# Adaptive max pooling on one core: a nine-row ring, 48 KB load runs, 9 KB store runs, and stores queued behind the last load

## The chip, the cores and the metric

One core of one Trainium2 chip. The metric is the device time of one execution in microseconds (us), lower is better. The profile's "span" is the time from the first to the last instruction of one profiled execution; it is 1.7 to 1.8 us shorter than the time of the same execution, so spans are compared with spans and times with times. All runs told here were in the fast state (none is set apart as slow by a lower clock or a longer time), at a granted clock of 1.0. A ratio is the mean time of one kernel's fast runs over that of the other's fast runs of the same rounds, so it is not quite the ratio of the medians quoted beside it.

## The reference

The input is float32 of 32 x 256 x 4096. Each row of 4096 is cut into 256 windows of 16, and each window gives its maximum:

```python
for i in range(output_size):                    # 256
    start = int(i * length / output_size)       # 16 * i
    end = int((i + 1) * length / output_size)
    result[:, :, i] = np.max(x[:, :, start:end], axis=-1)
```

There are 8192 rows, 64 for each of the 128 SBUF partitions. 134.2 MB are read and 8.39 MB written, with one pass of maxima over the input.

## The kernel before

A partition gets two consecutive rows per load (32 KB contiguous) in one of three buffers. VectorE reduces each row, and each pair of rows is stored (2 KB contiguous per partition). The first 14 stores go out on ScalarE's DMA queue when they are ready. The next 16 are deferred and put on SyncE's queue, the one that issues the loads, in groups of 6, 5 and 5. The last four rows are loaded in smaller pieces.

```python
R = 2; IN_BUFS = 3; CHUNKS_PER_ROW = 4; N_CHUNK_ROWS = 2; N_FULL_ROWS = 2
DEF_A, DEF_B, DEF_C = 6, 5, 5
xt = xf.rearrange("(n p r) (o w) -> n p r o w", p=P, r=R, w=W)
ot = of.rearrange("(n p r) m -> n p (r m)", p=P, r=R)
# ... pools and helpers cut ...
for n in range(n_body):                          # 30 loads of two rows
    t = in_pool.tile([P, R, O, W], fp32, tag="in")
    nc.sync.dma_start(out=t, in_=xt[n])
    o = new_out()
    for r in range(R):
        nc.vector.reduce_max(out=o[:, r * O : (r + 1) * O], in_=t[:, r],
                             axis=mybir.AxisListType.X)
    out_tiles[n] = o
    if n >= defer_start:
        deferred.append(n)
    else:
        nc.scalar.dma_start(out=ot[n], in_=o)
emit_deferred(DEF_A)
# ... two single-row loads; emit_deferred(DEF_B) ahead of the last two rows;
# ... these two rows in four pieces of 4 KB each; a store of rows 60, 61 ...
emit_deferred(len(deferred))
nc.scalar.dma_start(out=ot[last_n], in_=out_tiles[last_n])
```

Of the kernel before, what the change touches and what calls it, by code (L numbers as in the profile page):

```python
# [1 line left out]

# [4 lines left out]


@with_exitstack  # L10
def kernel(
    ctx: ExitStack,
    tc: tile.TileContext,
    x: bass.AP,
    output_size: bass.AP,
    out: bass.AP,
):
    nc = tc.nc

    B, C, L = x.shape  # L20
    O = int(output_size)
    assert L % O == 0, (L, O)
    W = L // O

    P = nc.NUM_PARTITIONS

    xf = x.flatten_outer_dims()
    of = out.flatten_outer_dims()
    rows = xf.shape[0]
    assert rows % P == 0  # L30

    fp32 = mybir.dt.float32

    R = 2
    IN_BUFS = 3
    CHUNKS_PER_ROW = 4
    N_CHUNK_ROWS = 2
    N_FULL_ROWS = 2
    DEF_A = 6
    DEF_B = 5  # L40
    DEF_C = 5

    while R > 1 and rows % (P * R) != 0:
        R //= 2
    nprow = rows // P
    nmacro = nprow // R
    n_chunks = CHUNKS_PER_ROW if O % CHUNKS_PER_ROW == 0 else 1
    oc = O // n_chunks

    n_tail_prow = min(N_CHUNK_ROWS + N_FULL_ROWS, nprow)  # L50
    n_chunk_prow = min(N_CHUNK_ROWS, n_tail_prow)
    n_tail_macro = -(-n_tail_prow // R)
    n_body = nmacro - n_tail_macro
    tail_start_prow = n_body * R
    n_defer = min(DEF_A + DEF_B + DEF_C, max(n_body - 1, 0))

    xt = xf.rearrange("(n p r) (o w) -> n p r o w", p=P, r=R, w=W)
    ot = of.rearrange("(n p r) m -> n p (r m)", p=P, r=R)

    in_pool = ctx.enter_context(tc.tile_pool(name="inpool", bufs=IN_BUFS))  # L60
    out_pool = ctx.enter_context(
        tc.tile_pool(name="outpool", bufs=min(nmacro, n_defer + 5))
    )

    out_tiles = {}
    deferred: list[int] = []

    def new_out():
        return out_pool.tile([P, R * O], fp32, tag="out", name="o")

    def emit_deferred(k):
        for _ in range(k):
            if deferred:
                m = deferred.pop(0)
                nc.sync.dma_start(out=ot[m], in_=out_tiles[m])  # L75

    defer_start = n_body - n_defer
    for n in range(n_body):
        t = in_pool.tile([P, R, O, W], fp32, tag="in")
        nc.sync.dma_start(out=t, in_=xt[n])  # L80
        o = new_out()
        for r in range(R):
            nc.vector.reduce_max(  # L83
                out=o[:, r * O : (r + 1) * O],
                in_=t[:, r],
                axis=mybir.AxisListType.X,
            )
        out_tiles[n] = o
        if n >= defer_start:
            deferred.append(n)  # L90
        else:
            nc.scalar.dma_start(out=ot[n], in_=o)

    emit_deferred(DEF_A)

    o = None
    last_n = nmacro - 1
    for q in range(tail_start_prow, nprow):
        n, r = divmod(q, R)
        if r == 0 or o is None:  # L100
            o = new_out()
            out_tiles[n] = o
        if q == nprow - n_chunk_prow:
            emit_deferred(DEF_B)
        if q < nprow - n_chunk_prow:
            tr = in_pool.tile([P, 1, O, W], fp32, tag="inrow", bufs=2)
            nc.sync.dma_start(out=tr, in_=xt[n][:, r : r + 1])
            nc.vector.reduce_max(  # L108
                out=o[:, r * O : (r + 1) * O],
                in_=tr[:, 0],  # L110
                axis=mybir.AxisListType.X,
            )
        else:
            for c in range(n_chunks):
                tl = in_pool.tile(
                    [P, oc, W], fp32, tag="inchunk", bufs=2 * n_chunks
                )
                nc.sync.dma_start(
                    out=tl, in_=xt[n][:, r, c * oc : (c + 1) * oc, :]
                )  # L120
                nc.vector.reduce_max(  # L121
                    out=o[:, r * O + c * oc : r * O + (c + 1) * oc],
                    in_=tl,
                    axis=mybir.AxisListType.X,
                )
        if r == R - 1 and n != last_n:
            nc.scalar.dma_start(out=ot[n], in_=o)

    emit_deferred(len(deferred))

    nc.scalar.dma_start(out=ot[last_n], in_=out_tiles[last_n])


# [1 line left out]
_INS = ['x', 'output_size']  # L135
_OUTS = [((32, 256, 256), 'float32')]
#: Inputs that are plain numbers.
_NUMBERS = {'output_size': 256}


# [26 lines left out]
```

## Time and profile before

| | kernel before |
|---|---|
| time, median of the first 3 runs | 339.17 us (338.6 to 339.9) |
| span of the profiled run | 336.9 us |
| VectorE (DVE) busy | 281.0 us, 83% |
| mean DMA rate over the span | 423 GB/s |
| data packets per DMA engine | 576 |

First the page of the kernel before. The row DMA has one digit for each fortieth of the span, the busy share of the 16 DMA engines in tenths; 9 is 90% or more.

```profile
span 336.9 us, 241 instructions
...
DVE 281.0 (83%) x70; POOL 0.2 (0%) x4
...
DMA  7999999999999999999999999999999999999997
...
DMA packets 10370, 142.63 MB, mean 423 GB/s; under 512 B 1152, under 2 KB 1152, under 8 KB 6272
...
L83 DVE TENSOR_REDUCE o<-t 128x256 f32<-128x4096 f32 x60 | 262.4, 4414 | 50.5 <-DMA t<-in_x_dram 50.5
```

The DMA row is full from end to end. The last line tells of VectorE: 60 reduces of 4414 ns, and 50.5 us of idle time, all ended by a load. VectorE waits for DMA.

Then the chain of waits of the kernel before, its summary line:

```profile
by line: DMA t<-in_x_dram 60.0%; DVE o L83 23.4%; DMA out_dram<-o 10.7%; DMA tl<-in_x_dram 2.8%; DVE o L121 0.7%; SPq L75 0.5%; SPq L80 0.3%; issue 0.3%; DVEq L83 0.0%
```

The chain puts 23.4% on VectorE, since each load waits for VectorE to free a buffer. But two more loads stand in the queue then, so the DMA engines don't stop. A chain shows what released what; it does not show that a queue between the two was full.

The windows of the end (bounds and length in us, busy time of VectorE and GpSimd, clock, DMA share, GB/s):

```profile
300.00:320.00 20.00, 18.08 (x5) 0.00 (x0) 1.00 0.99 401
320.00:330.00 10.00, 9.07 (x7) 0.00 (x0) 1.00 1.03 416
330.00:332.00 2.00, 1.96 (x2) 0.00 (x0) 1.00 1.04 402
332.00:334.00 2.00, 1.38 (x2) 0.00 (x0) 1.00 0.77 296
334.00:336.90 2.90, 0.00 (x0) 0.00 (x0) 1.00 0.27 102
```

In the last 5 us the engines run dry.

Each DMA packet has its own record in the trace (start, duration, size, queue). Grouped by size, for the kernel before ("sum" is over all packets, divided by 16 engines):

```
bytes   count   median ns   mean ns   sum us
 2048    4096       84         84.1    21.5
 4096    1024      159        160.3    10.3
16384     256      611        626.4    10.0
32768    3840     1213       1217.1   292.1
completion writes (4 bytes) 1152, 9 ns  0.6     all: 334.55 us
```

The medians lie on a line of 0.0368 ns per byte (0.03675 before rounding: 1213 less 84 ns over 30,720 bytes) plus 8 to 9 ns per packet. The first packet starts at 1.75 us and the last ends at 335.71 us.

### The profile page before, as it was taken

To read this page: it belongs to the slowest core of one execution; us is meant where nothing else is said; L and a number is where in the kernel's file an instruction comes from. 1 tells how busy PE (TensorE), PEld (TensorE's weight loads), DVE (VectorE), ACT (ScalarE), POOL (GpSimd) and SP (SyncE) were. 2 spreads that over 40 slices of the span, in tenths; PEclk is the share of its full clock that TensorE was granted. 3 is DMA by queue.
4 is the path that set the end of the run, shared out by engine and by line. 5 is a ranking of instruction groups with operands and counts; after the bars stand their busy time and mean duration, and the time that the engine had idled before them with its cause. 6 is when DMAs were issued, how large, how long until landed. Compare 5 with 4: busy or idle time off the path is not lost.

```text
span 336.9 us, 241 instructions
## 1 busy us (share of the span) xinstructions
DVE 281.0 (83%) x70; POOL 0.2 (0%) x4
## 2 busy tenths in 40 slices
DVE  0488988888988889888899888888988888898895
POOL 0000000000000000000000000000000000000000
DMA  7999999999999999999999999999999999999997
GB/s 311 436 436 441 417 454 406 454 409 454 426 430 430 436 428 434 430 430 435 429 438 432 436 432 436 436 436 428 424 436 428 436 412 436 429 414 427 405 414 275
DMA packets 10370, 142.63 MB, mean 423 GB/s; under 512 B 1152, under 2 KB 1152, under 8 KB 6272
## 3 DMA queue, kind: packets, MB, share of 16 engines
q1 hardware_dynamic: 8064, 138.42, 96.1%
q10 hardware_dynamic: 2304, 4.20, 3.2%
q14 instruction: 2, 0.02, 0.0%
HBM read 134.22 MB, written 8.39 MB: 423 GB/s over the span
## 4 chain that ended last, share of the span: by engine, by line
DMA 74%; DVE 24%; SPq 1%; issue 0%; DVEq 0%
DMA t<-in_x_dram 60%; DVE o L83 23%; DMA out_dram<-o 11%; DMA tl<-in_x_dram 3%; DVE o L121 1%; SPq L75 1%; SPq L80 0%; DVEq L83 0%
## 5 line engine op out<-in xcount | busy, mean ns | idle before, releaser
L83 DVE TENSOR_REDUCE o<-t 128x256 f32<-128x4096 f32 x60 | 262.4, 4414 | 50.5 <-DMA t<-in_x_dram 50.5
L121 DVE TENSOR_REDUCE o<-tl 128x64 f32<-128x1024 f32 x8 | 9.8, 1220 | 1.0 <-DMA tl<-in_x_dram 0.6
L108 DVE TENSOR_REDUCE o<-tr 128x256 f32<-128x4096 f32 x2 | 8.8, 4420 | 1.0 <-DMA tr<-in_x_dram 0.9
L148 POOL MEMSET const-bfloat16-1.0<- 128x1 bf16 x1 | 0.1, 102 | 0.0
L148 POOL MEMSET const-uint8-127<- 128x1 uint8 x1 | 0.1, 101 | 0.0
L148 POOL MEMSET const-float32-0.0<- 128x1 f32 x1 | 0.1, 99 | 0.2 <-issue 0.2
L148 POOL MEMSET const-float32-1.0<- 128x1 f32 x1 | 0.1, 98 | 0.0
## 6 DMA issues: line engine op xcount, KB each, us to landing
t<-in_x_dram SPq DMA_DIRECT2D x30, 4096.0 KB, 21.5
out_dram<-o ACTq DMA_DIRECT2D x16, 256.0 KB, 16.1
out_dram<-o SPq DMA_DIRECT2D x16, 256.0 KB, 14.0
tr<-in_x_dram SPq DMA_DIRECT2D x2, 2048.0 KB, 16.4
tl<-in_x_dram SPq DMA_DIRECT2D x8, 512.0 KB, 9.2
```

Of the source, the lines that this page charges most:

```text
L75: nc.sync.dma_start(out=ot[m], in_=out_tiles[m])
L83: nc.vector.reduce_max(out=o[:, r * O : (r + 1) * O], in_=t[:, r], axis=mybir.AxisListType.X,)
L108: nc.vector.reduce_max(out=o[:, r * O : (r + 1) * O], in_=tr[:, 0], axis=mybir.AxisListType.X,)
L121: nc.vector.reduce_max(out=o[:, r * O + c * oc : r * O + (c + 1) * oc], in_=tl, axis=mybir.AxisListType.X,)
L148: nc = _bacc.Bacc("TRN2", target_bir_lowering=False, num_devices=1)
```

## The change

The intent is fewer and larger DMA runs, with an end at which the queue holds work while VectorE finishes. Two-row buffers become a ring of nine rows filled three rows at a time (48 KB contiguous per partition). Two-row stores become nine-row stores (9 KB contiguous), seven of them. The last row, the 64th, goes in four pieces. Most group stores are held until after the last load. The words of the change say four groups; the condition holds groups 2 to 6, which is five stores.

```diff
-    R = 2
-    IN_BUFS = 3
-    CHUNKS_PER_ROW = 4
-    N_CHUNK_ROWS = 2
-    N_FULL_ROWS = 2
-    DEF_A = 6
-    DEF_B = 5
-    DEF_C = 5
+    RING = 9
+    G = 9
+    N_GROUPS = 7
+    LOAD = 3
+    LATE = [3, 2, 2, 1, 1]
+    HELD = 4
+    PIECES = 4
...  (pools: ring [P, 9, O, W], six output tiles [P, 9 * O], one last output)
+    xg = xf[0:main].rearrange("(g p r) (o w) -> g p r o w", p=P, r=G, w=W)
+    og = of[0:main].rearrange("(g p r) m -> g p (r m)", p=P, r=G)
...
+    for g in range(N_GROUPS):
+        o = outs[g % len(outs)]
+        sizes = LATE if g == N_GROUPS - 1 else [LOAD] * (G // LOAD)
+        r = 0
+        for n in sizes:
+            at = n_read % RING
+            nc.sync.dma_start(out=ring[:, at : at + n], in_=xg[g][:, r : r + n])
+            for i in range(n):
                 nc.vector.reduce_max(
+                    out=o[:, (r + i) * O : (r + i + 1) * O],
+                    in_=ring[:, at + i],
                     axis=mybir.AxisListType.X,
                 )
+            n_read += n
+            r += n
+        if g < N_GROUPS - 1 - HELD:
+            nc.scalar.dma_start(out=og[g], in_=o)
+        else:
+            held.append((og[g], o))
...  (the last row: four loads of 4 KB per partition, four reduces)
+    for dst, src in held:
+        nc.sync.dma_start(out=dst, in_=src)
+    nc.scalar.dma_start(out=ol, in_=last_out)
```

More of the change, by code (lines that the diff above doesn't have):

```diff
@@ L18 @@
     nc = tc.nc
+    P = nc.NUM_PARTITIONS
+    fp32 = mybir.dt.float32
     B, C, L = x.shape
@@ L23 @@
     W = L // O
-    P = nc.NUM_PARTITIONS
     xf = x.flatten_outer_dims()
@@ L29 @@
     rows = xf.shape[0]
-    assert rows % P == 0
-    fp32 = mybir.dt.float32
-    R = 2
-    IN_BUFS = 3
-    CHUNKS_PER_ROW = 4
-    N_CHUNK_ROWS = 2
-    N_FULL_ROWS = 2
-    DEF_A = 6
-    DEF_B = 5
-    DEF_C = 5
-    while R > 1 and rows % (P * R) != 0:
-        R //= 2
-    nprow = rows // P
-    nmacro = nprow // R
-    n_chunks = CHUNKS_PER_ROW if O % CHUNKS_PER_ROW == 0 else 1
-    oc = O // n_chunks
-    n_tail_prow = min(N_CHUNK_ROWS + N_FULL_ROWS, nprow)
-    n_chunk_prow = min(N_CHUNK_ROWS, n_tail_prow)
@@ L52 @@
-    n_tail_macro = -(-n_tail_prow // R)
-    n_body = nmacro - n_tail_macro
-    tail_start_prow = n_body * R
-    n_defer = min(DEF_A + DEF_B + DEF_C, max(n_body - 1, 0))
-    xt = xf.rearrange("(n p r) (o w) -> n p r o w", p=P, r=R, w=W)
-    ot = of.rearrange("(n p r) m -> n p (r m)", p=P, r=R)
-    in_pool = ctx.enter_context(tc.tile_pool(name="inpool", bufs=IN_BUFS))
-    out_pool = ctx.enter_context(
-        tc.tile_pool(name="outpool", bufs=min(nmacro, n_defer + 5))
-    )
-    out_tiles = {}
@@ L66 @@
-    deferred: list[int] = []
-    def new_out():
-        return out_pool.tile([P, R * O], fp32, tag="out", name="o")
-    def emit_deferred(k):
-        for _ in range(k):
-            if deferred:
-                m = deferred.pop(0)
-                nc.sync.dma_start(out=ot[m], in_=out_tiles[m])
-    defer_start = n_body - n_defer
-    for n in range(n_body):
-        t = in_pool.tile([P, R, O, W], fp32, tag="in")
-        nc.sync.dma_start(out=t, in_=xt[n])
-        o = new_out()
-        for r in range(R):
-            nc.vector.reduce_max(
-                out=o[:, r * O : (r + 1) * O],
-                in_=t[:, r],
-                axis=mybir.AxisListType.X,
-            )
-        out_tiles[n] = o
-        if n >= defer_start:
-            deferred.append(n)
-        else:
-            nc.scalar.dma_start(out=ot[n], in_=o)
@@ L94 @@
-    emit_deferred(DEF_A)
-    o = None
-    last_n = nmacro - 1
-    for q in range(tail_start_prow, nprow):
-        n, r = divmod(q, R)
-        if r == 0 or o is None:
-            o = new_out()
-            out_tiles[n] = o
-        if q == nprow - n_chunk_prow:
-            emit_deferred(DEF_B)
-        if q < nprow - n_chunk_prow:
-            tr = in_pool.tile([P, 1, O, W], fp32, tag="inrow", bufs=2)
-            nc.sync.dma_start(out=tr, in_=xt[n][:, r : r + 1])
-            nc.vector.reduce_max(
-                out=o[:, r * O : (r + 1) * O],
-                in_=tr[:, 0],
-                axis=mybir.AxisListType.X,
-            )
-        else:
-            for c in range(n_chunks):
-                tl = in_pool.tile(
-                    [P, oc, W], fp32, tag="inchunk", bufs=2 * n_chunks
-                )
-                nc.sync.dma_start(
-                    out=tl, in_=xt[n][:, r, c * oc : (c + 1) * oc, :]
-                )
+    assert rows == 64 * P
@@ new lines @@
+    RING = 9
[5 more added lines that the diff above has]
+    PIECES = 4
+    pool = ctx.enter_context(tc.tile_pool(name="pool", bufs=1))
+    ring = pool.tile([P, RING, O, W], fp32, tag="ring", name="ring")
+    outs = [
+        pool.tile([P, G * O], fp32, tag=f"out{i}", name=f"out{i}")
+        for i in range(N_GROUPS - 1)
+    ]
+    last_out = pool.tile([P, O], fp32, tag="lastout", name="lastout")
+    main = N_GROUPS * G * P
+    xg = xf[0:main].rearrange("(g p r) (o w) -> g p r o w", p=P, r=G, w=W)
@@ new lines @@
+    og = of[0:main].rearrange("(g p r) m -> g p (r m)", p=P, r=G)
+    xl = xf[main:rows].rearrange("p (o w) -> p o w", w=W)
+    ol = of[main:rows]
+    n_read = 0
+    held = []
+    for g in range(N_GROUPS):
[6 more added lines that the diff above has]
+            for i in range(n):
@@ L121 @@
                 nc.vector.reduce_max(
-                    out=o[:, r * O + c * oc : r * O + (c + 1) * oc],
-                    in_=tl,
+                    out=o[:, (r + i) * O : (r + i + 1) * O],
+                    in_=ring[:, at + i],
                     axis=mybir.AxisListType.X,
                 )
-        if r == R - 1 and n != last_n:
-            nc.scalar.dma_start(out=ot[n], in_=o)
-    emit_deferred(len(deferred))
-    nc.scalar.dma_start(out=ot[last_n], in_=out_tiles[last_n])
+            n_read += n
@@ new lines @@
+            r += n
[3 more added lines that the diff above has]
+            held.append((og[g], o))
+    at = n_read % RING
+    oc = O // PIECES
+    for c in range(PIECES):
+        cut = slice(c * oc, (c + 1) * oc)
+        nc.sync.dma_start(out=ring[:, at, cut], in_=xl[:, cut])
+        nc.vector.reduce_max(
+            out=last_out[:, cut], in_=ring[:, at, cut], axis=mybir.AxisListType.X
+        )
+    for dst, src in held:
+        nc.sync.dma_start(out=dst, in_=src)
```

## The prediction

> **What bounds it now.** The 16 DMA engines. The page's slices show DMA at 0.9 or more from the second slice to the last but one, at about 430 GB/s, in a span of 336.9 us. The trace's packet records, summed over 16 engines, give 334.6 us of packet time between the first packet at 1.75 us and the last end at 335.7 us. VectorE is busy 281.0 us (83%); its 52 us of waits end on loads: 4.41 us a row against 4.87 us of load (1217 ns a 32 KB packet, 8 per engine, two rows). VectorE's pieces in the chain of waits lie under queued loads and cost nothing.
>
> Packet medians by size are 84 ns (2 KB), 159 (4 KB), 611 (16 KB), 1213 (32 KB): 0.0368 ns per byte, which is 435 GB/s over 16 engines, plus 8 to 9 ns per packet. 435 GB/s is the fabric ceiling in the Trainium skill, DMA: Bandwidth & Descriptors, "Where 436 GB/s comes from"; the trace agrees. The same page, "Why small descriptors are slow", tells of a fixed overhead per packet, about 3 cycles; the trace shows 8 to 9 ns. So 142.6 MB need 327.7 us at the ceiling; only some 9 us of the span can be had.
>
> **What changes.** Bytes and vector work stay. Data packets per engine fall from 576 to 280:
> - loads: 152 of 48 KB, 16 of 32 KB, 16 of 16 KB, 32 of 4 KB, instead of 240 of 32 KB, 16 of 16 KB, 64 of 4 KB;
> - stores: 56 of 9 KB and 8 of 1 KB instead of 256 of 2 KB.
>
> Estimate from the line and the measured means: 48 KB 1820 ns, 9 KB 347, 1 KB 46. Sum per engine: 276.6 + 19.5 + 10.0 + 5.1 + 19.4 + 0.4 + 0.3 (semaphore writes) = 331.3 us, 3.2 us less. About 1.7 us comes from the stores. All of it is on the path, since the queue is never empty.
>
> The end: before, the last store is issued (333.4 us) when most DMA work is gone; about 1.5 us are lost there. After, five held stores (groups 2 to 6; 5.9 MB, 13.9 us) stand behind the last load. VectorE ends about 11 us after the last load lands (44.7 us of reduces against 33.9 us of loads), so its last small store joins a busy queue: about 0.5 us gained. Three slots of three rows keep a load queued (reduces 13.3 us, load 14.6 us); VectorE's later start (about 18 us) costs nothing.
>
> Less overlap of packets gives back about 0.8 us. Net: span about 334.0, 2.9 us less.
>
> **Prediction: 336.2 us, range 334.3 to 338.6.** Faster by over 2%: 0.02; within 2%: 0.95; slower by over 2%: 0.03.
>
> **Right or wrong, in the profile.** 48 KB packets near 1815 ns, 9 KB near 347; 4,480 data packets on the two hardware queues; DMA share 1.0 to the end; VectorE busy 281 us, waiting about 1.3 us per three-row load; held stores from about 319 to 333 us at over 425 GB/s; VectorE ending near 331 us.
>
> **What would make it wrong.** A 48 KB run cut into smaller packets (the loads' gain, about 1.5 us, gone); the pure store stretch running slower than mixed traffic (10% is 1.4 us); a gap because a ring load waits too long on VectorE, or the last group's store for its last reduce; the 144 KB pitch of partitions meeting memory less evenly than 32 KB.

## The result, and the profile after

The changed kernel takes 336.6 us (336.56 to 336.69, 4 runs), the kernel before 338.95 us in its 4 runs. The ratio is 0.9929, 95% interval 0.9914 to 0.9944: 0.7% faster, clear of noise and well under 2%. The forecast was 336.2, range 334.3 to 338.6.

The page of the changed kernel:

```profile
span 334.8 us, 174 instructions
...
DVE 278.8 (83%) x67; POOL 0.2 (0%) x4
...
DMA  9899999999998999899998999989999999999997
...
DMA packets 5041, 142.62 MB, mean 426 GB/s; under 512 B 560, under 2 KB 688, under 8 KB 1200
...
L65 DVE TENSOR_REDUCE out<-ring 128x256 f32<-128x4096 f32 x63 | 274.3, 4412 | 50.0 <-DMA ring<-in_x_dram 50.0
```

The same bytes travel in about half the packets; VectorE waits as long as before, for the same cause. The 8s in the DMA row are no idleness: a packet is counted in the slice in which it starts, and a 48 KB packet lasts 1.8 us of a slice of 8.4 us.

The chain of waits of the changed kernel, its summary and its last pieces (start, length, what):

```profile
by line: DMA ring<-in_x_dram 61.4%; DVE out L65 33.1%; issue 2.2%; DVE lastout L82 1.0%; DVEq L119 0.3%; DVEq L65 0.0%
...
315.54 8.73 DVE out L65 x2
324.27 1.13 DVEq L119
325.40 3.38 DVE lastout L82 x3
```

VectorE's share in the chain has grown to 34%, though it is not what limits; an experiment below settles that.

The same windows of the end, changed kernel:

```profile
300.00:320.00 20.00, 20.00 (x6) 0.00 (x0) 1.00 1.00 418
320.00:330.00 10.00, 8.78 (x5) 0.00 (x0) 1.00 1.01 428
330.00:332.00 2.00, 0.00 (x0) 0.00 (x0) 1.00 1.03 438
332.00:334.00 2.00, 0.00 (x0) 0.00 (x0) 1.00 0.34 130
334.00:334.80 0.80, 0.00 (x0) 0.00 (x0) 1.00 0.00 0
```

The held stores run from 318.4 us on, alone from 319.5 us when the last load has landed, at 428 to 438 GB/s, while VectorE works till 328.8 us. The last small store, issued at 328.81 us, joins a queue that still has almost 5 us of work.

Packets of the changed kernel: 48 KB x2432, median 1815 ns, mean 1823.9; 9 KB x896, median 347; 32 KB, 16 KB, 4 KB and 1 KB at 1216, 615, 161 and 46 ns. The span taken apart:

| us | before | after | difference | forecast |
|---|---|---|---|---|
| first packet starts | 1.75 | 1.74 | -0.01 | 0 |
| packet time, sum over engines / 16 | 334.55 | 331.90 | -2.65 | -3.2 |
| idle less overlap of packets | -0.59 | -0.01 | +0.58 | +0.3 |
| last packet to the end of the span | 1.20 | 1.15 | -0.05 | 0 |
| span | 336.92 | 334.78 | -2.13 | -2.9 |

The forecast column is that of the prediction. The third line is the elapsed time from the first packet to the last less the packet time. Below zero, records of neighbouring packets on an engine overlap by more than the engines stand idle.

### The profile page after: what moved, and what is told of

Read it like the earlier page. It is cut to its first block, busy times and chain, and to the rows that moved or that the text cites. A ratio compares the mean times of both kernels' runs of the same rounds, so it can differ in the third digit from the quotient of the medians.

```text
span 334.8 us, 174 instructions
## 1 busy us (share of the span) xinstructions
DVE 278.8 (83%) x67; POOL 0.2 (0%) x4
## 4 chain that ended last, share of the span: by engine, by line
DMA 61%; DVE 34%; issue 2%; DVEq 0%
DMA ring<-in_x_dram 61%; DVE out L65 33%; DVE lastout L82 1%; DVEq L119 0%; DVEq L65 0%
## 5 line engine op out<-in xcount | busy, mean ns | idle before, releaser
L65 DVE TENSOR_REDUCE out<-ring 128x256 f32<-128x4096 f32 x63 | 274.3, 4412 | 50.0 <-DMA ring<-in_x_dram 50.0
L82 DVE TENSOR_REDUCE lastout<-ring 128x64 f32<-128x1024 f32 x4 | 4.6, 1208 | 0.0
```

Of the source, the lines that this page charges most:

```text
L65: nc.vector.reduce_max(out=o[:, (r + i) * O : (r + i + 1) * O], in_=ring[:, at + i], axis=mybir.AxisListType.X,)
L82: nc.vector.reduce_max(out=last_out[:, cut], in_=ring[:, at, cut], axis=mybir.AxisListType.X)
```

## The experiments

Theory P: the gain is the number of packets, each with a fixed cost on engines that never stop. Rival T: the gain is the end, where held stores cover the last reduces. Rival V: VectorE is on the path, as the chain of waits suggests. Runs of one batch share a chip and the runs of the kernel before.

### The changed kernel again, and its packets multiplied

> The changed kernel unaltered, timed again as the yardstick for the other runs of its batch. Expected 336.6 us and a ratio to the kernel before of 0.993, within 0.2%.

Measured: 336.65 us (336.62 to 336.82, 5 runs), ratio 0.9939 (0.9925 to 0.9952), span 334.87. As expected. The kernel before had 338.82 us in this batch (338.57 to 340.24, 11 runs).

Stores in 1 KB runs, by padding each output row in SBUF so that rows don't join (abridged here, as the longer edits below; the lines that only follow from it are cut):

```diff
-        pool.tile([P, G * O], fp32, ...)
+        pool.tile([P, 9, O + 16], fp32, ...)
-            nc.scalar.dma_start(out=og[g], in_=o)        # held ones likewise
+            nc.scalar.dma_start(out=og[g], in_=o[:, :, 0:O])
```

> The changed kernel with the stores of its seven groups cut from 9 KB to 1 KB runs (padding in SBUF); bytes, number of store instructions, loads and order the same. Theory P (the gain is fewer packets, each with 8 to 9 ns of fixed time on a DMA engine that is never idle): 448 more packets per engine at 8.7 ns, so 3.9 us slower than the changed kernel, about 340.5 us, and slower than the kernel before. Theory T (the gain comes from the end of the program, where held stores cover the last reduces; run lengths don't matter): no change within 0.5 us, 336.6 us. 1 KB packets at 46 ns in both.

Measured: 339.59 us (339.43 to 339.73), ratio 1.0025 (1.0012 to 1.0037), span 337.94. That is 2.94 us over the changed kernel: slower than the kernel before, with the ring, the 48 KB loads and the held stores all in place. Rival T alone falls: the end was as in the changed kernel, and the gain was gone. Theory P has the direction and too large a size, 3.9 expected.

Loads in 16 KB runs, by the same means:

```diff
-    ring = pool.tile([P, RING, O, W], fp32, ...)
+    ring = pool.tile([P, RING, O + 1, W], fp32, ...)[:, :, 0:O]
```

> The changed kernel with one pad column block per ring row, so that each load moves 16 KB runs instead of 48 or 32 KB; same bytes, same 27 load instructions, same waits. Theory P: 320 more packets per engine at 8.7 ns, 2.8 us slower than the changed kernel, about 339.4 us. Theory T: within 0.5 us of 336.6. If 48 KB runs had a benefit or harm of their own (pitch, bursts), the difference would depart from 2.8 us by more than 1 us.

Measured: 338.61 us (338.42 to 339.32), ratio 0.9998 (0.9986 to 1.0011), span 337.04; 1.96 us over the changed kernel, 2.8 expected. 27 load instructions with the same waits carry the same bytes, and the whole gain is gone but for 0.2 us.

The sizes agree with each other to about 1 ns, though not with 8.7 ns:

| kernel | packets per engine | span us | over the changed kernel | per extra packet | the same by median times |
|---|---|---|---|---|---|
| changed, again | 280 | 334.87 | | | |
| loads in 16 KB | 600 | 337.04 | +2.16 | 6.8 ns | 6.1 ns |
| stores in 1 KB | 728 | 337.94 | +3.07 | 6.9 ns | 6.6 ns |
| kernel before | 576 | 336.92 | +2.04 | 6.9 ns | 7.3 ns |

The spans are of one profiled execution each (that of the kernel before is from the first batch), so their closer agreement is in part chance; the last column uses the medians of 5 and 11 times of this batch. What the runs carry is 6 to 7 ns per packet. The kernel before also differs in its end, so its row is no pure count of packets. Both paddings shift addresses in SBUF too; that was not tested apart from the packets.

The packet records tell why it is less than 8.7 ns. With 16 KB loads the packet time grows by 3.24 us, which is 320 packets at about 9 ns and their spread, yet the line "idle less overlap" falls from -0.01 to -1.18 us. Records that overlap in this way let a packet cost 6 to 7 ns net where its record shows 8 to 9 of fixed time.

### One part alone on the kernel before: 4 KB stores

```diff
+    S = 4
-    ot = of.rearrange("(n p r) m -> n p (r m)", p=P, r=R)
+    og = of[0:60*P].rearrange("(n p r) m -> n p (r m)", p=P, r=S)   # rows 0 to 59
-        nc.scalar.dma_start(out=ot[n], in_=o)              # each two rows
+        nc.scalar.dma_start(out=og[g], in_=o)              # each four rows
-    DEF_A = 6; DEF_B = 5; DEF_C = 5
+    DEF_A = 3; DEF_B = 2; DEF_C = 3
```

> The kernel before with its stores in groups of four rows (4 KB runs) instead of two (2 KB), for the first 60 of the 64 rows; the same 32 KB loads, the same tail of loads, stores held back at the same rows. Theory P: 120 fewer packets per engine at 8.6 ns, 1.0 us faster than the kernel before, about 337.9 us, ratio 0.997. Theory T: 0, ratio 1.000 within 0.1%.

Measured: 339.76 us (339.07 to 340.45), ratio 1.0028 (1.0014 to 1.0041), slower by 0.9 us where 1.0 us faster was expected. A miss. The profiled run was the fastest of the five (339.07 us, span 0.37 us longer than that of the kernel before), so its trace shows less than half of the 0.9 us. In it, packet time did fall, by 0.55 us (334.55 to 334.00), but "idle less overlap" rose by 0.94 us (-0.59 to +0.35). The waits of SyncE's queue show one of 6.0 us for a store to land, and the windows show the engines short of work after it:

```profile
SPq L83 <- DMA out_dram<-o: 6.0, 1, 6.0
```

```profile
330.00:333.00 3.00, 2.94 (x3) 0.00 (x0) 1.00 0.83 335
333.00:337.30 4.30, 0.38 (x1) 0.00 (x0) 1.00 0.39 152
```

ScalarE issued the store of rows 60 and 61 at 323.36 us; SyncE issued its next store only at 330.43 us, and it counts on the same completion semaphore. The run on the held stores, below, shows why that matters.

### VectorE nearly taken away, after and before

Each maximum over 4 of its 16 elements; the result is wrong, every transfer stays.

```diff
-                    in_=ring[:, at + i],
+                    in_=ring[:, at + i, :, 0:4],          # likewise for the last row
```

> The changed kernel with each maximum taken over 4 of its 16 elements: a wrong result on purpose, VectorE work about a quarter, every DMA the same. Theory P (DMA engines never idle, VectorE hidden, also at the end behind the held stores): 336.6 us, at most 0.4 us less. Rival V (VectorE is on the path, as the 34% in its chain of waits suggests): many us faster, at least 5.

Measured: 336.89 us (336.64 to 337.45), ratio 0.9944 (0.9933 to 0.9956). The page and the waits of this run:

```profile
DVE 74.7 (22%) x67; POOL 0.2 (0%) x4
```

```profile
DVE out L65 <- DMA ring<-in_x_dram: 243.1, 23, 17.9
```

VectorE works 204 us less and waits 193 us more, and the time does not fall. Rival V falls: the 34% of the chain bought nothing.

The same done to the kernel before:

> The kernel before with the same wrong quarter of VectorE work. Theory P: only the end is exposed, where its last small store waits for the last reduces: 0.5 to 1.5 us faster than the kernel before, that is 337.3 to 338.3 us. Rival V: 5 us faster or more.

Measured: 339.74 us (338.97 to 340.74, 6 runs), ratio 1.0029 (1.0014 to 1.0044): 0.95 us slower with less to do, where a gain of 0.5 to 1.5 us was expected. So the gain that my reading of the end promised, that the last store of the kernel before is late because of the last reduces, did not come. The profiled run is the slowest of the six (340.74 us), so its trace shows about 2 us of loss, twice that of the median. Its windows, and a wait of SyncE's queue:

```profile
320.00:330.00 10.00, 2.13 (x6) 0.00 (x0) 1.00 1.01 351
330.00:339.00 9.00, 1.26 (x3) 0.00 (x0) 1.00 0.71 251
```

```profile
SPq L118 <- DMA out_dram<-o: 6.7, 5, 5.5
```

The engines are busy at 351 GB/s. 155 of the 4 KB load packets between 320 and 333 us took over 30 ns more than the line gives, 2.0 us per engine in all; in the kernel before 11 did, for 0.07 us (325 to 330 us). At that place 4 KB loads and 2 KB stores alternate. Why that went so badly here is not shown. The run also brought a delay of its own: for 5.5 us SyncE could not issue a load, because ScalarE's store of rows 60 and 61, issued at 320.07 us, counts on the same completion semaphore (explained under the held stores, below). The last two loads were issued at 327.31 and 328.05 us, against 321.44 and 322.71 in the kernel before, and the last store at 334.58 against 333.43. So the run does not settle whether the last reduces cost the kernel before anything.

### Fewer stores behind the last load

```diff
-    HELD = 4
+    HELD = 0          # and HELD = 2
```

> The changed kernel with only the last group's store behind the last load (groups 0 to 5 stored as they finish); packets, bytes and VectorE work the same. Theory P plus tail: loads end 11.1 us later (four stores of 2.78 us come before them), VectorE ends 9.3 us after the last load, the last store needs about 3 us more: span about 343, 8 us slower than the changed kernel, about 344.8 us. If the held stores were of no use (theory of packets alone): 336.6 us.

Measured: 342.54 us (342.39 to 342.59, 4 runs), ratio 1.0108 (1.0094 to 1.0123): 5.9 us over the changed kernel of the first experiments, which ran on another chip.

> The changed kernel with three group stores behind the last load instead of five. Three stores are 8.3 us of DMA work against the 9.3 us that VectorE needs after the last load, and about 3 us for the last store: 2.5 to 3 us slower than the changed kernel, about 339.3 us, slower than the kernel before by 0.5 us. Packets alone: 336.6 us.

Measured: 338.76 us (338.53 to 338.84, 4 runs), ratio 0.9997 (0.9984 to 1.001): 2.1 us over the same. The order of sizes is right, both were forecast somewhat too large. The windows of the run with only one store held:

```profile
320.00:325.00 5.00, 5.00 (x3) 0.00 (x0) 1.00 0.97 410
325.00:330.00 5.00, 5.00 (x3) 0.00 (x0) 1.00 0.92 366
330.00:335.00 5.00, 5.00 (x3) 0.00 (x0) 1.00 0.14 59
335.00:340.80 5.80, 3.16 (x3) 0.00 (x0) 1.00 0.44 178
```

VectorE works without a gap while the DMA engines have nothing left. Here VectorE is on the path, and less so with three stores held ("idle less overlap" 5.93 us here and 1.98 us there, -0.01 in the changed kernel). Loads of three rows put VectorE 9.3 us behind the last load; the held stores, 13.9 us of transfers, pay for that. They are the condition under which the larger loads gain anything.

### Held stores alone, on the kernel before

```diff
-    DEF_A = 6; DEF_B = 5; DEF_C = 5
+    DEF_A = 0; DEF_B = 0; DEF_C = 16
```

> The kernel before with one part of the change alone: all sixteen held stores queued behind the last load, none between the last loads. Same packets, same VectorE work. Theory M (the end of the kernel before loses time because its small last loads and its stores share the engines, and because its queue is nearly empty when the last store comes): 0.4 to 1.0 us faster than the kernel before, about 338.1 us, and runs within 0.4 us of each other, where those of the kernel before spread over 1.3 us or more. Packets alone: no change, same spread.

Measured: 339.86 us (339.75 to 340.0), ratio 1.0034 (1.0021 to 1.0046), against 338.70 us (338.48 to 339.22) of the kernel before in this batch: 1.2 us slower, a miss. The spread was as expected, 0.25 us. SyncE's waits and the windows:

```profile
SPq L75 <- DMA out_dram<-o: 6.5, 5, 5.0
```

```profile
318.00:330.00 12.00, 12.00 (x9) 0.00 (x0) 1.00 1.04 405
330.00:334.00 4.00, 0.60 (x1) 0.00 (x0) 1.00 0.35 133
334.00:338.20 4.20, 0.00 (x0) 0.00 (x0) 1.00 0.71 267
```

The built program and the trace explain the hole at 330 to 334 us. A completion semaphore is a counter that a transfer raises when it has landed. Transfers of both queues take theirs in turn from a set of eight, in the order of the built program, in which ScalarE's last store stands before several of the held ones. One of the sixteen held stores gets the semaphore (number 103) of ScalarE's last small store, so SyncE may not issue it until that store has landed. ScalarE issues its store at 330.63 us, after the last reduce; SyncE's previous store was issued at 327.27 us, the one with number 103 follows at 332.66 us and four more after it. Meanwhile the queue drains. The kernel before has the same kind of wait at its end, of 4.9 us: ScalarE's store of rows 60 and 61 at 322.67 us and SyncE's store at 329.27 us count on the same semaphore, and three stores stand behind it. There the queue did not drain at once: the engines' share stays at 1.03 from 320 to 330 us. The changed kernel has five held stores and the last one; none comes round to ScalarE's semaphore, and its stores never wait for a store.

Longer stores on top of it (both edits together):

> The kernel before with all held stores behind the last load and stores in groups of four rows (4 KB runs). Theory P with the net cost of a packet from the earlier batch (6.7 ns in span): 120 fewer packets per engine, 0.8 us faster than the run with the stores behind the last load alone, about 337.3 us. If longer store runs have no value by themselves, no difference between the two; if they harm, as the single part seemed to, slower by about 0.9 us.

Measured: 338.92 us (338.51 to 339.07), ratio 1.0003 (0.999 to 1.0015). Against the run before it, 0.94 us less (span 1.31 less); 0.8 was expected for 120 packets. The idle hole of this run sits elsewhere (326 to 328 us), so the difference is not packets alone: of the 1.31 us of span, packet time is 0.55 and "idle less overlap" 1.00. The direction that the first 4 KB run seemed to deny is there, its size is not shown.

### Towards a faster version

```diff
-    LATE = [3, 2, 2, 1, 1]
-    HELD = 4
-    PIECES = 4
+    LATE = [3, 3, 3]
+    HELD = 5
+    PIECES = 1
```

> The changed kernel with its last row loaded in one piece instead of four, its last group in three loads of three rows instead of five smaller ones, and six group stores held behind the last load instead of five. 40 fewer packets per engine at 6.7 ns: 0.27 us faster, about 336.35 us. Cost, if any: VectorE ends about 13 us after the last load, covered by 16.7 us of held stores, so none.

Measured: 336.53 us (336.49 to 336.64), ratio 0.9935 (0.9921 to 0.9948). That is 0.1 us below the changed kernel on another chip (336.65, ratio 0.9939), less than the 0.27 expected. Packet time fell by 0.52 us, and 0.34 us of it came back as less overlap and more idleness at the end. It has 163 instructions for 174 and is at least level, but 0.1 us across two chips does not show it to be faster.

With its one early store issued by SyncE instead of by ScalarE (at 60.45 us instead of 60.09, so that it stands behind two queued loads and does not alternate with them):

```diff
-            nc.scalar.dma_start(out=og[g], in_=o)
+            early = (og[g], o)       # nc.sync.dma_start after the next group's loads
```

> As the run before it, with the one early group store issued from the same queue as the loads, in their order, instead of from ScalarE's queue. If the 0.4 to 0.5 us of slow 48 KB packets near 60 us come from packets of two queues alternating on an engine, it is 0.3 to 0.5 us faster than the run before it, about 335.9 us; if they come from writing among reads at all, no difference within 0.15 us.

Measured: 337.38 us (337.18 to 337.72), ratio 0.9961 (0.9949 to 0.9974), against 336.53 us on the same chip: 0.85 us slower, where 0.3 to 0.5 us faster or no change was expected. A miss for both readings. Some 16 load packets at the very start are slow in every run. Beyond these, with the store on ScalarE's queue, 56 load packets between 60 and 80 us took over 30 ns more than the line gives, 0.5 us per engine in all, while the store's own packets ran from 64 to 80 us. With the store on SyncE's queue 24 did, for 1.1 us: 20 started from 85.7 to 88.3 us, before the store's first packet, and four from 95.1 to 95.8 us; the store's packets ran from 90 to 94 us. So the spell goes where the store goes, and is no smaller in the loads' own queue. The Trainium skill, DMA: Bandwidth & Descriptors, "Queues, rings and completion order", says that each engine goes round-robin between the queues at packet granularity (a packet there is a group of descriptors); such alternation cannot be the whole cause here, since the spell (24 slow packets) stays when there is nothing to alternate with. What it is stays open. (It is not every store among loads: the changed kernel's second early store, at 110 to 125 us, brought no such spell, and of the six early stores of the run with one store held only the first did; the other five had two slow packets.)

## Why the prediction was right

The bound. "The 16 DMA engines" is shown: VectorE's work cut by 204 us made the changed kernel no faster, and packets put back made it slower. The Trainium skill, DMA: Bandwidth & Descriptors, "Where 436 GB/s comes from", gives the ceiling of 435 GB/s; the held stores ran at 428 to 438 in the windows shown (a packet counts whole in the window where it starts, so a window of 2 us can show more than the ceiling), the body of both kernels at about 432, so the ceiling holds here, and only 9 us of 337 lay above it.

The mechanism. Fewer packets is shown as the main cause: adding packets back to the changed kernel, in loads or in stores, costs 6 to 7 ns each, and 296 of them come to 1.8 to 2.1 us of the 2.13 us of span. The converse was not shown cleanly: 120 packets fewer in the kernel before came out 0.9 us slower once and 0.94 us faster once, with waits that differ in both.

The sizes. The terms of the sum were off. "Sum per engine ... 3.2 us less" measured 2.65, nearly all because 48 KB packets averaged 1823.9 ns and not 1820 (152 per engine, 0.6 us), of which 0.5 us (by all packets between 60 and 80 us) sits in the slow spell beside the first store. "Less overlap of packets gives back about 0.8 us" and "about 0.5 us gained" at the end came to 0.3 us of loss together and measured 0.58. With the packet records cut where the engines' share first falls below 1 at the end (333 us before, 332 us after), the overlap gave back 1.2 us and the end gained 0.6. So packet time and overlap were mis-sized, both in the same direction, and the gain in span, 2.9 us, was forecast 0.8 us too large. That the time missed by only 0.4 us is luck: 336.2 us fits 2.9 us taken from the median of 339.17 us, but the profiled run of the kernel before, with a span of 336.9 us, corresponds to 338.6 or 338.7 us. A net cost of 6 to 7 ns for the record's 8.7, and nothing else, would have given a gain of 1.8 to 2.1 us; the records of one kernel don't show the net cost unless their overlap is counted.

The end. "Its last small store joins a busy queue" is shown by the windows and by the runs with fewer held stores. That the end of the kernel before was late because of its reduces was not confirmed: with short reduces it was not faster, but that run had a delay of its own. What the trace shows there is that the last load landed at 331.83 us, the last store went out at 333.43 us after the last reduces, and SyncE stood waiting 4.9 us before for a store to land, on a semaphore that both queues use. How much each of these has of the 0.6 us less idle time at the end was not measured alone: the one run that held back all stores of the old kernel ran into that wait itself.

VectorE. Busy 278.8 us for 281 forecast, end at 328.8 us for "near 331"; its waits were mostly 1.45 us a load for 1.3. Nothing hung on these.

A thing not forecast is steadiness. The kernel before spread over up to 1.7 us within a batch, the changed kernel over at most 0.2 us. Holding its stores back brought the old kernel's spread to 0.25 us too (0.56 us with 4 KB stores on top), which agrees with mixed small loads and stores at its end as the cause, but does not prove it; the changed kernel with 16 KB loads spread over 0.9 us.

## What to carry to other kernels

When DMA engines are full, divide the bytes by the ceiling first, then count packets: what is left to win is the fixed cost per packet, the start and the end, and you can measure the cost per packet by padding a buffer until its runs break apart. Larger loads make the computing engine finish later after the last load, so queue enough finished stores behind that load to cover it, in few transfers, so that none has to wait for the semaphore of the very last one. Don't judge an engine by its share in the chain of waits: make its work smaller and see whether the time moves.

## What the Trainium skill lacked or had wrong

- DMA: Bandwidth & Descriptors, "Why small descriptors are slow (HBM only)": it gives about 3 cycles of fixed overhead per packet, and calls grouping consecutive descriptors into packets worth it only at 256 B or less. Here a packet record has 8 to 9 ns of fixed time and costs 6 to 7 ns net; on a full queue that decides between 16 KB and 48 KB loads (1.96 us of 336.65). The runs lengthened the contiguous runs themselves; grouping of descriptors was not tested.
- The same page, "Where 436 GB/s comes from": it says that transfers between HBM and SBUF are bound at about 358 GB/s. This core alone moved 423 to 426 GB/s over the whole span. HBM Reference, "Specifications (TRN2)", has about 425 GB/s for a core that streams alone, and agrees.
- No page looked up has the slow spell beside a store among loads: 24 to 56 slow load packets, 0.5 to 1.1 us per engine in the three runs counted here, in one queue or in two; nor the slow first load packets, about 16 in each run, 0.6 to 0.7 us per engine.
- No page looked up warns that an issuing queue can stand still because it shares rotating completion semaphores with another queue: waits of 4.9 to 6.8 us for a store to land in five of the runs, and in one of them the engines at a share of 0.35 for 4 us.
